# A strided read moves from VectorE and ACT to TensorE: the gated unit of a two-layer trunk

## The chip, the core and the metric

The kernel runs on one core of a Trainium2 chip. The metric is device time in microseconds (us) of one execution. TensorE (PE in the rows; its weight loads PEld) multiplies matrices, VectorE (DVE), ACT and GpSimd (POOL) work on elements, and SyncE (SP) issues most of the DMAs. A tile has 128 partitions and lies in SBUF; results of TensorE come out in PSUM banks of 512 float32 columns.

## What is computed

The program is two residual layers on a (1024 frames, 1024 channels) float32 input. The change is in the first layer, behind its state-space mixer. There `y` is the mixer's output and `gate` the second half of the input projection:

```python
y = jax.nn.gelu(y)
y = y * jax.nn.sigmoid(y @ s5_w_glu[j] + s5_b_glu[j])
out = (y * jax.nn.silu(gate)) @ s5_w_out[j]
x = x + out
```

The second line is the gated unit. Its product with `s5_w_glu` is 1024 x 1024 x 1024, and so is the product with `s5_w_out` that follows.

## The kernel before

Channels lie on partitions, in eight tiles of 128 channels (`KT` = 8), with the 1024 frames in the columns. A float32 matrix product is made of three products of rounded halves: each operand is split into `hi`, its value rounded to the type that TensorE takes at full rate, and `lo`, the rest. `mm3` issues hi by hi, hi by lo and lo by hi as three matmuls of 512 moving columns into one PSUM bank.

The mixer works on chunks of `L` = 8 frames, so it leaves y in another order of columns: in `bh[k]` and `bl[k]` (hi and lo of channel tile k; `hi` and `lo` in the rows) column l*128 + c holds frame c*8 + l. The input `zt` (the gate, stored by frames) and the results `ahi` and `alo` (hi and lo of what goes into the product with `s5_w_out`) are in order of frames, column c*8 + l.

The gated unit is the loop over `i` in 0..7 below (lines 1017 to 1037), each turn with two halves of 512 columns. A half here is l = 0..3 or l = 4..7 with all 128 chunks. One half adds `bh` and `bl` to `yv`, multiplies by silu of the gate (a Sigmoid on ACT and two multiplications on VectorE), takes 24 matmuls in `project` over the eight channel tiles with a slice of `w_glu` as stationary operand, puts a Sigmoid on the bank (ACT), multiplies, rounds to `ahi` (ACT) and subtracts to `alo` (VectorE). `of_frames` is a view of a tile in order of frames that walks it in steps of 8 columns, 32 bytes: it is read for the gate (one ACT and one VectorE instruction), written for `ahi` (ACT), and read and written for `alo` (VectorE). TensorE reads `bh` and `bl` as 512 adjacent columns. `sig`, `zt` and `yv` are `c` in the rows, and `bglu` is the bias.

Before this loop lie the input projection (`mm<-ahi,w_hi` and the like), the mixer and `y_split`, which splits each y tile into `bh` and `bl` half by half. Behind it comes `load_panel`: four DMAs of 512 KB bring a panel of `s5_w_out` into `raw` (two buffers), ACT and VectorE split it into the tiles that held `bh` and `bl`, and `apply_panel` multiplies it with slices of `ahi` and `alo` (`mm<-hi,ahi` in the rows). Up to the loop, instructions keep the order in which they are written; from the loop on a scheduler orders them for each engine. Every engine works its queue in order. All compute instructions are recorded under line 74, the helper that issues them, so they are told apart by tiles.

Of the kernel before, what the change touches and what calls it, by code (L numbers as in the profile page):

```python
# [18 lines left out]
F32 = mybir.dt.float32  # L19
F32R = mybir.dt.float32r  # L20
I32 = mybir.dt.int32
AF = mybir.ActivationFunctionType
ALU = mybir.AluOpType
# [5 lines left out]
KT = D // P  # L29
# [3 lines left out]
L = 8  # L33
# [27 lines left out]
def trunk(ctx, tc, x, norm_g, final_g, s5_w_in, A_re, A_im, log_dt, B_re, B_im, C_re, C_im,  # L61
# [17 lines left out]
    V, S, GP, T, Q = (Engine(e) for e in (nc.vector, nc.scalar, nc.gpsimd, nc.tensor, nc.sync))  # L79
# [20 lines left out]
    def mmps():  # L100
        return bank("mm")

    def auxps():
        return bank("aux")
# [9 lines left out]
    def mm3(ps, a, b, first, last):  # L114
        (ah, al), (bh, bl) = a, b
        T.matmul(ps, lhsT=ah, rhs=bh, start=first, stop=False)
        T.matmul(ps, lhsT=ah, rhs=bl, start=False, stop=False)
        T.matmul(ps, lhsT=al, rhs=bh, start=False, stop=last)

    def sub_hi(eng, lo, src, hi):  # L120
        eng.tensor_tensor(lo, src, hi.bitcast(F32), ALU.subtract)
# [27 lines left out]
    def load_w(src, col0, lo_eng=None, raw=None):  # L149

        if raw is None:
            raw = raw_tile([P, KT, P])
        Q.dma_start(raw, src[:, col0:col0 + P].rearrange("(k p) c -> p k c", p=P))
        hi = wsp.tile([P, KT, P], F32R, name="w_hi", tag="hi")
        lo = wsp.tile([P, KT, P], F32R, name="w_lo", tag="lo")
        S.activation(hi, raw, AF.Copy)
        sub_hi(lo_eng or V, lo, raw, hi)
        return hi, lo

    def project(ps, w, a, half):  # L160
        hi, lo = w
        mh, ml = a
        cs = slice(half * HALF, (half + 1) * HALF)
        for k in range(KT):
            mm3(ps, (hi[:, k], lo[:, k]), (mh(k)[:, cs], ml(k)[:, cs]), k == 0, k == KT - 1)
# [27 lines left out]
    ahi = A.tile([P, KT, D], F32R, name="ahi")  # L193
    alo = A.tile([P, KT, D], F32R, name="alo")
# [495 lines left out]
    b_pool, bh, bl = [], {}, {}  # L690
    c_n = [0]

    def ctile(dt=F32, shape=(P, D)):
        c_n[0] += 1
        return b_pool[1].tile(list(shape), dt, name="c", tag=f"c{c_n[0] % 8}")
# [7 lines left out]
    def b_lo(k):  # L703
        return bl[k]

    def by_l(a):
        return a.rearrange("p (l c) -> p l c", l=L // 2)

    def of_frames(a, half):

        return a.rearrange("p (c l) -> p l c", l=L)[:, half * (L // 2):(half + 1) * (L // 2)]

    def load_y(k):
        bl[k] = btile(k, "lo")
# [301 lines left out]
    b_ops = (b_hi, b_lo)  # L1016
    banks.update(mm=[0, 1, 2, 3], aux=[4, 5, 6, 7])
    for i in range(KT):
        w = w_next
        if i < KT - 1:  # L1020
            w_next = load_w(w_glu[0], (i + 1) * P)
        sig, zt, yv = ctile(), ctile(), ctile()
        Q.dma_start(zt, z_d[i])
        for half in range(2):
            hs = slice(half * HALF, (half + 1) * HALF)

            zs = of_frames(zt, half)
            V.tensor_tensor(yv[:, hs], bh[i][:, hs].bitcast(F32), bl[i][:, hs].bitcast(F32), ALU.add)
            S.activation(by_l(sig[:, hs]), zs, AF.Sigmoid)
            V.tensor_tensor(by_l(yv[:, hs]), by_l(yv[:, hs]), zs, ALU.mult)  # L1030
            V.tensor_tensor(yv[:, hs], yv[:, hs], sig[:, hs], ALU.mult)
            ps = mmps()
            project(ps, w, b_ops, half)
            S.activation(sig[:, hs], ps, AF.Sigmoid, bias=bglu[:, i:i + 1])
            V.tensor_tensor(yv[:, hs], yv[:, hs], sig[:, hs], ALU.mult)
            S.activation(of_frames(ahi[:, i], half), by_l(yv[:, hs]), AF.Copy)
            V.tensor_tensor(of_frames(alo[:, i], half), by_l(yv[:, hs]), of_frames(ahi[:, i], half).bitcast(F32), ALU.subtract)


    gb = late.tile([P, D], F32, name="gb", tag="gb")  # L1040
# [37 lines left out]
    for half in range(2):  # L1078
        hs = slice(half * HALF, (half + 1) * HALF)
# [5 lines left out]
        for n in range(KT):  # L1085
            ps = mmps()
# [39 lines left out]
    for q in range(2):  # L1126
        ps = auxps()
# [11 lines left out]
    for q in range(2):  # L1139
        ps = auxps()  # L1140
# [6 lines left out]
    for half in range(2):  # L1147
# [10 lines left out]
        for n in range(KT):  # L1158
            ns = slice(n * P, (n + 1) * P)
            ps = mmps()  # L1160
# [19 lines left out]
    for h in range(8):  # L1180
        w = w_next
# [4 lines left out]
        for half in range(2):  # L1186
            hs = slice(half * HALF, (half + 1) * HALF)
            ps = mmps()
# [3 lines left out]
            ps = auxps()  # L1192
# [15 lines left out]
    for half in range(2):  # L1208
        hs = slice(half * HALF, (half + 1) * HALF)
# [6 lines left out]
        for n in range(KT):  # L1216
            ps = mmps()
# [39 lines left out]
```

## Time and profile before

| | us |
|---|---|
| time, median of 3 runs (848.52 to 853.45) | 850.79 |
| the profiled execution's own time | 851.53 |
| its span, first to last instruction | 849.8 |
| TensorE busy | 821.2 (97%) |
| VectorE busy | 495.9 (58%) |
| ACT busy | 293.6 (35%) |
| gated unit on TensorE: 384 matmuls | 275.4 to 366.0 |

The span is the time from the first to the last instruction; the profiled time is 1.7 us above it. Busy time of an engine is an average over stages with different limits. The stage of the gated unit is read by a window of its own, from 275.4 to 366.0 us, with the windows on either side of it. In a window's row each engine has its busy time and the count of its instructions, and PEclk is the granted clock of TensorE as a share of full speed.

A matmul's own duration (about 0.4 us) holds the filling and draining of the array, which overlap with its neighbours. What one matmul costs in a stream is the distance from its start to the next one's start.

### The profile page before, as it was taken

How to read it: one execution, taken by the hardware profiler on the slowest of the kernel's cores; microseconds unless marked ns; L12 is line 12 of the kernel's file. 1: busy time of each engine (PE TensorE's matmuls, PEld its weight loads, DVE VectorE, ACT ScalarE, POOL GpSimd, SP SyncE). 2: the span in 40 equal slices, each digit the busy share in tenths (PEclk: the TensorE clock that was granted, in tenths of full speed). 3: DMA queues.
4: the chain of work that ended last, by engine and by line, in shares of the span. 5: the costliest groups of instructions: out<-in, count | busy, mean ns of one | idle time of the engine just before them, and what ended most of it. 6: DMA issues, size and time to landing. Idle time of an engine off the chain costs nothing.

```text
span 849.8 us, 10879 instructions
## 1 busy us (share of the span) xinstructions
PE 821.2 (97%) x3978; PEld 668.1 (79%) x3978; DVE 495.9 (58%) x1035; ACT 293.6 (35%) x519; POOL 192.0 (23%) x197
## 2 busy tenths in 40 slices
PE   7999899999999999989999999999999999999996
PEld 5776688888887788758888888888888888888884
DVE  7889788888625978773177311221398545452255
ACT  5632444444423755563122321311321222332122
POOL 2059777787520000000000000000000112113221
PEclk9999899999999999999999999999999999999998
DMA  9826787878987723374021221200310112270022
GB/s 276 113 74 181 177 224 201 206 203 203 240 181 196 223 75 124 123 224 149 0 99 75 99 75 49 100 25 1 99 51 1 29 46 93 99 250 5 0 100 99
DMA packets 123573, 101.72 MB, mean 120 GB/s; under 512 B 21504, under 2 KB 104448, under 8 KB 123520
## 3 DMA queue, kind: packets, MB, share of 16 engines
q1 hardware_dynamic: 113040, 94.41, 39.9%
q10 hardware_dynamic: 10480, 6.62, 2.5%
q8 instruction: 31, 0.51, 0.3%
q14 instruction: 22, 0.18, 0.1%
HBM read 66.93 MB, written 25.17 MB: 108 GB/s over the span
## 4 chain that ended last, share of the span: by engine, by line
PE 60%; DVE 14%; DMA 10%; ACT 5%; POOL 4%; issue 3%; SPq 3%; DVEq 0%; ACTq 0%; POOLq 0%
PE mm L74 55%; DVE c L74 4%; PE aux L74 4%; SPq L74 3%; DMA raw<-in_s_w_in 3%; ACT c L74 2%; DMA lo<-y_d 2%; DVE stage L74 1%; DVE w_lo L74 1%; DMA t_d<-kpad 1%; DVE rot L74 1%; POOL w_lo L74 1%; DMA raw<-in_s_w_out 1%; ACT w_hi L74 1%; DVE wn L74 1%
## 5 line engine op out<-in xcount | busy, mean ns | idle before, releaser
L74 PE MATMUL mm<-ahi,w_hi 128*128 128x512 f32 x512 | 210.0, 410 | 5.9 <-DVE stage L74 4.4
L74 PE MATMUL mm<-alo,w_hi 128*128 128x512 f32 x512 | 202.7, 396 | 0.0
L74 PE MATMUL mm<-ahi,w_lo 128*128 128x512 f32 x512 | 195.7, 395 | 0.0
L74 PEld LDWEIGHTS mm<-ahi,w_hi 128*128 128x128 f32 x512 | 96.9, 189 | 27.9 <-DVE stage L74 5.7
L74 PEld LDWEIGHTS mm<-ahi,w_lo 128*128 128x128 f32 x512 | 96.7, 189 | 21.4
L74 PEld LDWEIGHTS mm<-alo,w_hi 128*128 128x128 f32 x512 | 97.2, 190 | 19.9 <-DVE alo L74 2.2
L74 DVE TENSOR_TENSOR w_lo<-raw,w_hi 128x1024 fp32r<-128x1024 f32 x28 | 40.8, 1456 | 69.0 <-ACT w_hi L74 69.0
L74 PE MATMUL mm<-c,ahi 128*128 128x512 f32 x256 | 80.4, 396 | 0.0
L74 POOL TENSOR_TENSOR c<-c,hi 128x512 f32<-128x512 f32 x16 | 21.0, 1311 | 258.9 <-ACT c L74 258.9
L74 ACT ACTIVATE w_hi<-raw 128x1024 fp32r<-128x1024 f32 x38 | 40.1, 1056 | 76.1 <-PE mm L74 56.2
L74 DVE TENSOR_TENSOR c<-mm,c 128x512 f32<-128x512 f32 x32 | 21.9, 690 | 65.7 <-PE mm L74 65.7
L74 PEld LDWEIGHTS mm<-c,ahi 128*128 128x128 f32 x256 | 48.0, 188 | 11.5
L74 PE MATMUL mm<-hi,ahi 128*128 128x512 f32 x128 | 51.4, 402 | 3.4 <-ACT hi L74 2.8
L74 POOL TENSOR_SCALAR_AFFINE_SELECT wsn<-wsn 128x1024 f32<-128x1024 f32 x1 | 1.1, 1091 | 230.3 <-DMA wsn<-in_sgu_w_s 230.3
L74 PE MATMUL mm<-hi,w_hi 128*128 128x512 f32 x128 | 50.7, 396 | 1.6 <-ACT w_hi L74 1.6
L74 PE MATMUL mm<-lo,ahi 128*128 128x512 f32 x128 | 51.6, 403 | 0.5 <-DVE lo L74 0.5
L74 PE MATMUL mm<-hi,alo 128*128 128x512 f32 x128 | 51.7, 405 | 0.0
L74 DVE TENSOR_TENSOR c<-c 128x512 f32<-128x512 f32 x64 | 49.5, 815 | 3.2 <-POOL c L74 3.1
L74 PE MATMUL mm<-hi,w_lo 128*128 128x512 f32 x128 | 50.6, 397 | 0.3 <-DVE w_lo L74 0.3
L74 PE MATMUL mm<-ahi,hi 128*128 128x512 f32 x128 | 50.7, 396 | 0.0
L74 PE MATMUL mm<-lo,w_hi 128*128 128x512 f32 x128 | 50.6, 396 | 0.0
L74 PE MATMUL mm<-alo,hi 128*128 128x512 f32 x128 | 50.6, 395 | 0.0
(174 smaller groups left out, 1438.4 us busy)
## 6 DMA issues: line engine op xcount, KB each, us to landing
raw<-in_sgu_w_in SPq DMA_DIRECT2D x24, 512.0 KB, 3.7
cs<-e SPq DMA_DIRECT2D x32, 256.0 KB, 3.9
raw<-in_s_w_in SPq DMA_DIRECT2D x14, 512.0 KB, 5.8
u_d<-stage SPq DMA_DIRECT2D x8, 512.0 KB, 5.3
us<-u_d SPq DMA_DIRECT2D x16, 256.0 KB, 5.2
t_d<-kpad SPq DMA_DIRECT2D x64, 64.0 KB, 3.0
traw<-t_d SPq DMA_DIRECT2D x16, 256.0 KB, 4.9
y_d<-ysb ACTq DMA_DIRECT2D x16, 256.0 KB, 3.3
```

Of the source, the lines that this page charges most:

```text
L74: ins = getattr(self.engine, name)(*args, **kwargs)
```

## The change

The frames are now put in order where TensorE reads y. `frames(a, half)` views a y tile as 64 chunks of 8 frames, the innermost step being 128 columns (512 bytes): a half is now 512 frames in sequence, chunks 0..63 or 64..127 with all eight l. The sum `yv`, the gate, the Sigmoids, the bank, `ahi` and `alo` all lie in order of frames, in adjacent columns. The addition reads `bh` and `bl` with the step of 128 columns. Every one of the 384 matmuls of the loop has such a view as its moving operand; the weights and the output bank stay as they were.

```diff
-    def by_l(a):
-        return a.rearrange("p (l c) -> p l c", l=L // 2)
-
-    def of_frames(a, half):
-
-        return a.rearrange("p (c l) -> p l c", l=L)[:, half * (L // 2):(half + 1) * (L // 2)]
+    def frames(a, half):
+
+        return a.rearrange("p (l c) -> p c l", l=L)[:, half * 64:(half + 1) * 64]
+
+    def by_c(a):
+        return a.rearrange("p (c l) -> p c l", l=L)
...
-            zs = of_frames(zt, half)
-            V.tensor_tensor(yv[:, hs], bh[i][:, hs].bitcast(F32), bl[i][:, hs].bitcast(F32), ALU.add)
-            S.activation(by_l(sig[:, hs]), zs, AF.Sigmoid)
-            V.tensor_tensor(by_l(yv[:, hs]), by_l(yv[:, hs]), zs, ALU.mult)
+            V.tensor_tensor(by_c(yv[:, hs]), frames(bh[i].bitcast(F32), half), frames(bl[i].bitcast(F32), half), ALU.add)
+            S.activation(sig[:, hs], zt[:, hs], AF.Sigmoid)
+            V.tensor_tensor(yv[:, hs], yv[:, hs], zt[:, hs], ALU.mult)
             V.tensor_tensor(yv[:, hs], yv[:, hs], sig[:, hs], ALU.mult)
             ps = mmps()
-            project(ps, w, b_ops, half)
+            for k in range(KT):
+                mm3(by_c(ps), (w[0][:, k], w[1][:, k]), (frames(bh[k], half), frames(bl[k], half)), k == 0, k == KT - 1)
             S.activation(sig[:, hs], ps, AF.Sigmoid, bias=bglu[:, i:i + 1])
             V.tensor_tensor(yv[:, hs], yv[:, hs], sig[:, hs], ALU.mult)
-            S.activation(of_frames(ahi[:, i], half), by_l(yv[:, hs]), AF.Copy)
-            V.tensor_tensor(of_frames(alo[:, i], half), by_l(yv[:, hs]), of_frames(ahi[:, i], half).bitcast(F32), ALU.subtract)
+            S.activation(ahi[:, i, hs], yv[:, hs], AF.Copy)
+            sub_hi(V, alo[:, i, hs], yv[:, hs], ahi[:, i, hs])
```

On TensorE the order of the 384 matmuls is the same in both kernels. It first differs where they end and the panel begins. The names are `hi0` to `hi7` for the panel's tiles by channel tile, and one `mm` for each tile of 128 frames:

```order
 L74 MATMUL mm_3508<-hi7_2925,w_lo_3394 128x512
 L74 MATMUL mm_3581<-hi0_2763,ahi_80 128x512
+L74 MATMUL mm_3609<-hi0_2763,ahi_80 128x512
+L74 MATMUL mm_3637<-hi0_2763,ahi_80 128x512
 L74 MATMUL mm_3581<-lo0_2514,ahi_80 128x512
 L74 MATMUL mm_3581<-hi0_2763,alo_81 128x512
 L74 MATMUL mm_3581<-hi1_2785,ahi_80 128x512
+L74 MATMUL mm_3609<-lo0_2514,ahi_80 128x512
+L74 MATMUL mm_3609<-hi0_2763,alo_81 128x512
 L74 MATMUL mm_3581<-lo1_2589,ahi_80 128x512
 L74 MATMUL mm_3581<-hi1_2785,alo_81 128x512
 L74 MATMUL mm_3581<-hi2_2812,ahi_80 128x512
```

Work of the second and third tile of frames (`mm_3609`, `mm_3637`) now stands among that of the first, before the panel's later tiles are asked for.

On ACT, at the same place, before (`c<-mm,bglu` is a Sigmoid that empties a bank of the gated unit, `hi_2763` to `hi_2925` are the panel's eight tiles):

```order
L74 ACTIVATE c<-mm,bglu 128x512
L74 ACTIVATE hi_2763<-raw 128x512
L74 ACTIVATE hi_2785<-raw 128x512
L74 ACTIVATE ahi<-c 128x4x128
L74 ACTIVATE hi_2812<-raw 128x512
L74 ACTIVATE hi_2835<-raw 128x512
L74 ACTIVATE c<-mm,bglu 128x512
L74 ACTIVATE hi_2856<-raw 128x512
```

and after:

```order
L74 ACTIVATE c<-mm,bglu 128x512
L74 ACTIVATE hi_2763<-raw 128x512
L74 ACTIVATE hi_2785<-raw 128x512
L74 ACTIVATE ahi<-c 128x512
L74 ACTIVATE hi_2812<-raw 128x512
L74 ACTIVATE hi_2835<-raw 128x512
L74 ACTIVATE c<-mm,bglu 128x512
L74 ACTIVATE hi_2856<-raw 128x512
```

The rows stand alike, but before there is one more Sigmoid of the gated unit behind them, and after these two are the last ones: the panel's first copies have moved one half behind, and `ahi` is written in one run of 512 columns.

## Rows read from the trace of the kernel before

**Rows 1.** The page: engine, busy us (share of the span), instructions.
```profile
PE 821.2 (97%) x3978; PEld 668.1 (79%) x3978; DVE 495.9 (58%) x1035; ACT 293.6 (35%) x519; POOL 192.0 (23%) x197
```

**Rows 2.** Windows: start:end, length, busy us (instructions) by engine, granted clock, DMA.
```profile
255.00:275.40 20.40, 18.82 (x81) 14.93 (x79) 10.79 (x18) 6.23 (x11) 0.00 (x0) 1.00 0.74 190
275.40:366.00 90.60, 90.22 (x384) 71.94 (x385) 75.81 (x89) 54.40 (x62) 0.00 (x0) 1.00 0.44 137
366.00:381.00 15.00, 11.06 (x37) 7.11 (x36) 10.00 (x14) 8.32 (x14) 0.00 (x0) 0.89 0.76 246
```

**Rows 3.** Timeline of PE: start us, us, instruction [idle before <- releaser]. Gated unit.
```profile
275.46 0.49 PE L74 MATMUL mm<-hi,w_hi 128*128 128x512 f32 x1 [1.64 <-ACT w_hi L74]
...
278.44 0.40 PE L74 MATMUL mm<-hi,w_hi 128*128 128x512 f32 x1
...
281.01 0.39 PE L74 MATMUL mm<-hi,w_lo 128*128 128x512 f32 x1
```

**Rows 4.** VectorE by shapes, 262 to 385 us: busy us, mean ns, idle before.
```profile
L74 DVE TENSOR_TENSOR alo<-c,ahi 128x512 fp32r<-128x512 f32 x16 | 20.6, 1286 | 6.4 <-ACT ahi L74 6.2
L74 DVE TENSOR_TENSOR w_lo<-raw,w_hi 128x1024 fp32r<-128x1024 f32 x8 | 9.8, 1222 | 18.5 <-ACT w_hi L74 18.5
L74 DVE TENSOR_TENSOR lo<-raw,hi 128x512 fp32r<-128x512 f32 x14 | 9.0, 688 | 6.4 <-ACT hi L74 6.4
L74 DVE TENSOR_TENSOR c<-hi,lo 128x512 f32<-128x512 f32 x13 | 8.5, 689 | 0.2
```

**Rows 5.** ACT by shapes, 262 to 385 us.
```profile
L74 ACT ACTIVATE ahi<-c 128x512 fp32r<-128x512 f32 x16 | 19.9, 1243 | 35.9 <-DVE c L74 35.9
L74 ACT ACTIVATE c<-c 128x512 f32<-128x512 f32 x16 | 19.1, 1257 | 0.0
L74 ACT ACTIVATE w_hi<-raw 128x1024 fp32r<-128x1024 f32 x8 | 8.5, 1059 | 11.0 <-DMA raw<-in_s_w_glu 11.0
L74 ACT ACTIVATE hi<-raw 128x512 fp32r<-128x512 f32 x14 | 8.1, 626 | 8.6 <-DMA raw<-in_s_w_out 8.6
```

**Rows 6.** VectorE: gate's multiplications, 281 to 285 us; input projection's evictions (min/median/max ns), strided, contiguous.
```profile
L74 DVE TENSOR_TENSOR c<-c 128x512 f32<-128x512 f32 x3 | 3.6, 1224 | 0.0
...
L74 DVE TENSOR_TENSOR stage<-mm,rb x13: 664/1132/1183, 63.7 to 171.7; 128x512 f32<-128x512 f32 x13
...
L74 DVE TENSOR_TENSOR stage<-mm,rb x13: 665/680/692, 187.6 to 280.8; 128x512 f32<-128x512 f32 x13
```

**Rows 7.** Timeline behind the gated unit: the first panel's matmuls and what they wait for.
```profile
368.16 0.50 PE L74 MATMUL mm<-lo,ahi 128*128 128x512 f32 x1 [0.30 <-DVE lo L74]
...
371.66 1.15 ACT L74 ACTIVATE hi<-raw 128x512 fp32r<-128x512 f32 x2 [3.92 <-DMA raw<-in_s_w_out]
...
372.34 0.51 PE L74 MATMUL mm<-hi,ahi 128*128 128x512 f32 x1 [2.76 <-ACT hi L74]
...
373.06 0.65 PE L74 MATMUL mm<-lo,ahi 128*128 128x512 f32 x1 [0.22 <-DVE lo L74]
373.51 0.63 PE L74 MATMUL mm<-hi,alo 128*128 128x512 f32 x1
...
375.22 0.63 PE L74 MATMUL mm<-hi,ahi 128*128 128x512 f32 x1
...
376.70 0.40 PE L74 MATMUL mm<-hi,ahi 128*128 128x512 f32 x1
...
379.61 0.50 PE L74 MATMUL mm<-hi,ahi 128*128 128x512 f32 x1 [0.66 <-ACT ahi L74]
```

**Rows 8.** Timelines at the loop's start: the last y tiles' splits on ACT and VectorE.
```profile
275.31 3.22 ACT L74 ACTIVATE hi<-lo 128x512 fp32r<-128x512 f32 x6
...
278.39 2.49 DVE L74 TENSOR_TENSOR lo<-lo,hi 128x512 fp32r<-128x512 f32 x4
```

## The prediction

> **What bounds the kernel now.** I read the page's table of engines first: TensorE is busy 97% of the span, VectorE 58%, ACT 35% [rows 1]. An average doesn't say which engine sets the end of the gated unit, so I read three windows next [rows 2]. In the stage of 90.60 us TensorE is busy for 90.22 with 384 matmuls at full granted clock (PEclk 1.00, the upper level, 2.4 GHz); VectorE is busy for 75.81 and ACT for 54.40. So TensorE is the bound there: 0.4 us of the stage is left to win by making the others faster. Behind it, from 366 to 381 us, TensorE has 3.9 us without work and a granted clock of 0.89. The timeline of TensorE gives the price of one matmul [rows 3]: from the start at 278.44 to the one at 281.01 us lie eleven steps, 2.57 / 11 = 0.2336 us for 512 columns, or 0.456 ns a column. 384 x 0.2336 = 89.7 us is the stage. Whatever the change does to this one number is multiplied by 384; all else in it happens on engines with slack.
>
> **The change part by part.** *VectorE and ACT lose strides.* Groups of one operation with and without a step of 8 columns show what a stride costs them. VectorE's subtraction to `alo` takes 1286 ns, the same subtraction on adjacent columns 688 [rows 4]; the multiplication by the gate takes 1224 [rows 6]. ACT's rounding to `ahi` takes 1243 and the gate's Sigmoid 1257, against 626 on adjacent columns [rows 5]. The change takes from VectorE 16 x (1.286 - 0.688) + 16 x (1.224 - 0.688) = 18.1 us, and from ACT 16 x 0.617 + 16 x 0.631 = 20.0 us. It gives VectorE a stride in the 16 additions of `bh` and `bl`, now 689 ns [rows 4]; at the excess of 0.6 us just seen that is 9.6 us back. No row has a step of 128 columns; from 0.45 us (the evictions below) to twice 0.6 for two strided inputs, 7 to 19 us, so VectorE's own balance is between -11 and +1 us. None of this is on the path within the stage, because TensorE fills it: the price of these edits there is nothing, and TensorE's 90.22 us is the cover. It shows only at the two ends of the stage.
>
> *The end of the stage.* The waits of TensorE behind it are 0.30, 2.76, 0.22 and 0.66 us, 3.9 together, the longest for a panel tile that ACT could copy only when a DMA of `s5_w_out` had landed [rows 7]. After the 2.76 us without work matmuls start about 0.43 us apart (373.51 to 375.22, four steps), which is the lower level of 1.2 GHz, until the row at 376.70: nine steps from 372.34 in 4.36 us against 2.1 at full clock, of which 0.2 is a wait already counted, so 2.0 more. Together up to 5.9 us. The panel's tiles overwrite the y tiles, so ACT may copy one only once TensorE has read that y tile for the last time. If TensorE reads y slowly, the DMAs run ahead of it and these waits nearly go; I take -5 us, from bounds of 0 and -5.9. The order shown ahead, in which work of a second and third tile of frames fills the wait for the later panel tiles, points the same way.
>
> *The start.* A half now needs both halves of every y tile. The last tiles are split until 275.31 + 3.22 = 278.53 on ACT and 278.39 + 2.49 = 280.88 on VectorE [rows 8], and TensorE comes to the eighth tile 21 matmuls after 275.46, at about 280.4. That is 0 to 0.5 us of new waiting, and nothing when matmuls take longer.
>
> *TensorE gains a stride.* This decides. All moving operands of TensorE in the kernel before are adjacent columns, so no row shows the price of 512 columns at a step of 128. What rows show is the price of a strided column on the two other engines. ACT: 512 columns more cost 1059 - 626 = 433 ns, 0.85 ns a column, and the stride adds 617 or 631 ns on 512, so 2.05 or 2.08 ns a strided column [rows 5]. VectorE: (1222 - 688) / 512 = 1.04 ns a column, plus 598 / 512 = 1.17, so 2.21 ns; for the gate's multiplication 1.04 + 536 / 512 = 2.09 [rows 4, 6]; for the evictions of the input projection, the same operation in two layouts, 1.04 + (1132 - 680) / 512 = 1.93 [rows 6]. Two engines whose adjacent columns differ by a fifth (0.85 and 1.04) meet at about 2 ns when each column is fetched apart. The rows look like a time of the memory and not of the engine. If so, TensorE pays it too: 512 x 1.93 to 512 x 2.21 is 0.988 to 1.132 us for a matmul instead of 0.2336. Of these I take the lowest, 1.93, since TensorE is the fastest reader here (0.456 ns). The term is 384 x (0.988 - 0.2336) = 290 us; with 2.21 it is 345.
>
> The Trainium skill ("SBUF — State Buffer", section "Door 1: The DMA port swizzle") says that the memory has lines of 16 bytes, that full bandwidth wants at least two accesses in a row to one line, and that each step to a new line pays. That it pays, the rows of VectorE and ACT bear out; the size of the penalty and TensorE's part in it the page doesn't give. Read with this case's rate, four adjacent columns to a line, 4 x 0.456 = 1.82 ns a line and one line a column, it would make a matmul 0.934 us, an estimate, and the kernel 851.5 + 384 x 0.700 - 5 = 1115 us.
>
> **The sum.** Against the profiled execution's own 851.5 us: + 290 (384 matmuls) - 5 (end of the stage) + 0 (start) = 1136 us. The median of the runs is 0.7 us lower than that execution, which does not count here.
>
> **The rivals.**
> *A, the forecast: a time per fetched column.* 1136 us at 1.93 ns, 1191 at 2.21, 1197 without the gain at the end. For it: two engines with different rates meet at the same nanoseconds. Against it: TensorE may have a wider path to the memory than the other two.
> *B, a factor.* A strided column costs each engine a multiple of its own adjacent column: 1.93 / 1.04 = 1.85 to 2.08 / 0.85 = 2.45 in the rows above. Then a matmul takes 0.432 to 0.572 us, the stage gains 76 to 130 us, and the kernel takes 923 to 977 us, near 945 at 2.1. For it: both engines lose roughly half their rate. Against it: the factors differ (2.0 and 2.45) where the nanoseconds agree.
> *C, a sum.* The stride adds a fixed excess to the instruction, 0.452 to 0.631 us in the rows; 384 of them are 174 to 242 us, and the kernel takes 1020 to 1089. It fits the same rows, but a matmul is pipelined with the next, so an addition that ignores the engine's own rate is the least natural of the three.
> *D, not slower: TensorE takes strided columns at its own rate.* The place is the moving operand of the 384 matmuls, the price 0 per column. The 90.6 us stage stays, the stage's end gives 0 to 5.9 us, the start takes up to 0.5, and the kernel takes 846 to 852 us, 849 in the middle. It decides from a matmul longer by less than 5.9 / 384 = 0.015 us, 6%. For it: nothing in the trace shows TensorE limited by its operand's layout. Against it: the only two engines seen with strides both pay, and TensorE asks for a column twice as often as they do. The Trainium skill ("TensorE: Matmul & The Clock Gate", section "Step-by-step: what each phase is for") states such a rule: throughput is purely the number of columns, one fed in each cycle. The trace agrees for adjacent columns to within a tenth, 0.456 ns against a cycle of 0.417; no run here shows it for strided ones.
>
> That the change doesn't do what it says holds in part: VectorE still has 16 strided instructions of its former 32. It would move the time only in D.
>
> **How the numbers follow.** A 50%, B 25%, C 8%, D 15%, and 2% for something outside, such as a step of 128 columns costing far more than one of 8. The predicted time is A's. The range goes from B's lower end to A's upper, 923 to 1197 us; it holds A, B and C, 83%. About 0.5%, 4.3 us, is what a measurement of this kernel can tell from no change. A, B and C are slower by far more, 85% with the rest. D is split by its own bounds: most of 846 to 852 lies within 4.3 us of 850.8, so 11% for no change and 4% for faster.
>
> **What would show it.** Right: the distance between starts of the 384 matmuls near 1 us, the stage near 380 us, TensorE still the one without idle time in it, `alo<-c,ahi` near 690 ns and both ACT groups near 630 on the engines that now wait for TensorE, the addition `c<-hi,lo` near 1.2 us, and the waits behind the stage nearly gone. A distance of 0.43 to 0.57 us is B, 0.69 to 0.87 is C, 0.234 is D. A granted clock below 1.00 in the stage would mean that TensorE, waiting for columns, is also throttled; where the memory sets the rate it changes nothing, and in B it would hide as a doubling. The forecast is wrong if TensorE fetches several strided columns at once.

## The result, and the profile after

The changed kernel takes 941.37 us (median; 937.82 to 941.49) against 850.98 us before: a ratio of 1.1059, 95% interval 1.1033 to 1.1085. It is slower, as forecast, by 90 us and not by 285: the time of rival B. The profiled execution took 937.82 us, 1.7 more than its span of 936.1; the other three took 941.35 to 941.49.

The page's table of engines and three windows of the changed kernel, which answer to [rows 1, 2] (columns as there):

```profile
PE 914.1 (98%) x3978; PEld 676.9 (72%) x3978; DVE 489.2 (52%) x1035; ACT 278.0 (30%) x519; POOL 192.2 (21%) x197
...
255.00:272.12 17.12, 17.12 (x77) 14.05 (x75) 10.34 (x14) 4.96 (x10) 0.00 (x0) 1.00 0.70 188
272.12:459.08 186.96, 186.96 (x385) 80.33 (x384) 70.97 (x94) 42.05 (x63) 0.00 (x0) 1.00 0.24 76
459.08:474.00 14.92, 14.92 (x65) 12.03 (x64) 7.49 (x12) 6.28 (x13) 0.00 (x0) 1.00 0.53 178
```

All of the 90 us and more lies in the middle row. The gated unit takes 186.96 us where it took 90.60, at a granted clock of 1.00 in both, with TensorE busy throughout. In the rows on either side TensorE has no idle time now, where before it had 1.6 and 3.9 us.

The timeline of TensorE in that stage gives the price of a matmul, as in [rows 3]:

```profile
272.12 0.71 PE L74 MATMUL mm<-hi,w_hi 128*128 128x512 f32 x1
...
278.53 0.69 PE L74 MATMUL mm<-hi,w_lo 128*128 128x512 f32 x1
...
283.89 0.69 PE L74 MATMUL mm<-lo,w_hi 128*128 128x512 f32 x1
```

From 278.53 to 283.89 lie eleven steps: 0.487 us for a matmul, 2.08 times the 0.2336 of before, and 0.951 ns a column. 384 x (0.487 - 0.2336) = 97 us.

VectorE and ACT, by shapes from 262 to 475 us (answers to [rows 4, 5]):

```profile
L74 DVE TENSOR_TENSOR c<-hi,lo 128x512 f32<-128x512 f32 x12 | 15.4, 1320 | 0.2
L74 DVE TENSOR_TENSOR alo<-c,ahi 128x512 fp32r<-128x512 f32 x16 | 10.9, 684 | 2.1 <-ACT ahi L74 1.4
...
L74 ACT ACTIVATE ahi<-c 128x512 fp32r<-128x512 f32 x16 | 10.3, 646 | 13.9 <-DVE c L74 13.9
L74 ACT ACTIVATE c<-c 128x512 f32<-128x512 f32 x16 | 9.1, 631 | 0.0
```

Their strides are gone and their instructions take half as long, except the addition of hi and lo, which took the stride over (689 to 1320 ns).

The account against the profiled execution of before: the stage from its first to its last matmul +96.4 (186.96 against 366.06 - 275.46 = 90.60); ahead of it -3.3 (it begins at 272.12, not 275.46, of which 1.64 is the wait in [rows 3]); behind it -6.7 (477.0 us from its end to the end of the span, before 483.7). Together +86.3, and the spans differ by 936.1 - 849.8 = 86.3. The -3.3 ahead of the stage belongs to this execution more than to the change: its first matmul of the input projection begins at 11.0 us and not at 12.4, in code that both kernels share, and the other three executions are 3.5 us longer.

### The profile page after: what moved, and what is told of

It is laid out like the page before. It is cut to its first block, busy times and chain, and to the rows that moved or that the text cites. A ratio compares the mean times of both kernels' runs of the same rounds, so it can differ in the third digit from the quotient of the medians.

```text
span 936.1 us, 10879 instructions
## 1 busy us (share of the span) xinstructions
PE 914.1 (98%) x3978; PEld 676.9 (72%) x3978; DVE 489.2 (52%) x1035; ACT 278.0 (30%) x519; POOL 192.2 (21%) x197
## 4 chain that ended last, share of the span: by engine, by line
PE 80%; DVE 7%; DMA 5%; POOL 4%; ACT 2%; SPq 1%; issue 1%; DVEq 0%; ACTq 0%; POOLq 0%
PE mm L74 75%; PE aux L74 4%; DMA raw<-in_s_w_in 2%; SPq L74 1%; DVE gg L74 1%; DVE rot L74 1%; POOL w_lo L74 1%; DVE stage L74 1%; POOL hh L74 1%; DMA cs<-e 1%; POOL e L74 1%; POOL et L74 1%; POOL s L74 1%; DVE tv L74 1%; DVE t L74 1%
## 5 line engine op out<-in xcount | busy, mean ns | idle before, releaser
L74 PEld LDWEIGHTS mm<-ahi,w_lo 128*128 128x128 f32 x512 | 96.4, 188 | 21.1
L74 PE MATMUL mm<-lo,w_hi 128*128 128x512 f32 x128 | 88.1, 689 | 0.0
L74 PE MATMUL mm<-hi,w_hi 128*128 128x512 f32 x128 | 88.1, 688 | 0.0
L74 PE MATMUL mm<-hi,w_lo 128*128 128x512 f32 x128 | 87.9, 688 | 0.0
L74 DVE TENSOR_TENSOR c<-c 128x512 f32<-128x512 f32 x64 | 41.8, 682 | 59.8 <-ACT c L74 56.6
L74 PEld LDWEIGHTS mm<-hi,w_lo 128*128 128x128 f32 x128 | 26.8, 209 | 35.5 <-issue 35.2
L74 PEld LDWEIGHTS mm<-lo,w_hi 128*128 128x128 f32 x128 | 26.8, 209 | 35.4 <-issue 35.1
L74 PEld LDWEIGHTS mm<-hi,w_hi 128*128 128x128 f32 x128 | 26.8, 209 | 35.3 <-issue 35.3
```

Of the source, the lines that this page charges most:

```text
L74: ins = getattr(self.engine, name)(*args, **kwargs)
```

## The experiments

Where a kernel below mixes columns of the product with the gate of other frames, its output is not the reference's; its work has the same size, and only its time is used. `pe_only`, `cold` and the eight kernels with other steps and runs were executed once each; the kernel before scattered from 848 to 853 us.

**Which half of the change costs.** One kernel strides TensorE's reads alone, another eases VectorE and ACT alone.

```diff
 # pe_only, from the kernel before
-            project(ps, w, b_ops, half)
+            for k in range(KT):
+                mm3(by_c(ps), (w[0][:, k], w[1][:, k]), (frames(bh[k], half), frames(bl[k], half)), k == 0, k == KT - 1)
...
 # elem_only, from the changed kernel
-            for k in range(KT):
-                mm3(by_c(ps), (w[0][:, k], w[1][:, k]), (frames(bh[k], half), frames(bl[k], half)), k == 0, k == KT - 1)
+            project(ps, w, b_ops, half)
```

> The kernel before, with the 384 matmuls of the gated unit reading y in steps of 128 columns as in the changed kernel; VectorE and ACT keep their views in steps of 8 columns (so columns of the product and of the gate no longer belong to the same frame). Theory 1, the loss is TensorE's reading alone: starts of matmuls 0.4865 us apart as in the changed kernel, 384 x (0.4865 - 0.2336) = 97 us on the stage, and a time of 937 to 945 us, because VectorE and ACT, strided or not, hide under a stage of 187 us. Rival: their work matters still, and with their strides kept the time is longer than the changed kernel's by part of the 30 us that they save, 945 to 970 us.

> The changed kernel, with the 384 matmuls reading 512 adjacent columns as before; VectorE and ACT keep the changed kernel's views (so the product's columns are in another order than the gate's). Theory 1, TensorE alone carries the loss and the eased engines give back only the waits at the two ends of the stage: matmuls 0.2336 us apart and 843 to 850 us. Rival: the eased engines give nothing, since the end waits for a DMA of the panel anyway: 850 to 853 us. A second rival, that the changed kernel's other edits cost time: above 854 us.

Measured: 943.54 us with TensorE's stride alone, and 843.73 us with the other half alone, ratio 0.9918 (0.9896 to 0.9941). So the loss is TensorE's reading, all of it. Strided or not, VectorE and ACT make no difference that can be seen under a stage of 187 us: the span of `pe_only` is 5.7 us longer than that of the changed kernel's profiled execution (941.8 against 936.1), and its stage begins 5.65 us later (277.77 against 272.12), 2.4 of them a wait for the first weights, so that nothing is left for the stage and what follows. Without TensorE's stride their relief is worth 0.8%. Window 366 to 381 us of the second kernel, where the kernel before had 11.06 us of work in 15 [rows 2]:

```profile
366.00:381.00 15.00, 15.00 (x66) 12.06 (x65) 8.61 (x14) 7.03 (x14) 0.00 (x0) 1.00 0.76 243
```

66 matmuls in the time of 37, at full clock: the 6.3 us that the kernel gained (849.98 to 843.73) are the waits behind the stage and the half clock that followed them, up to 5.9 us in the prediction's count.

**A time or a factor.** The changed kernel with TensorE made idle ahead of the stage:

```diff
     w_next = in_w[16]
+    for _ in range(8):
+        S.activation(w_next[0], w_next[0].bitcast(F32), AF.Copy)
```

> The changed kernel, with eight more copies of the first weight tile onto itself on ACT ahead of the gated unit (8 x 1.06 us), so that TensorE sits idle for some 8 us and begins its strided matmuls at the lower granted clock, 1.2 GHz. Theory E, the price belongs to TensorE and scales with its clock: the first matmuls start 0.97 us apart, twice 0.4865, and fall to 0.4865 once the clock is back. Theory M, the price is a time of the memory, 0.95 ns a column: they start 0.4865 us apart, or a little more, from the first one on, at half clock too. The total is 8 to 10 us over the changed kernel under M, 2 to 6 us more under E.

Measured: 948.99 us, 7.6 over the changed kernel's median. Windows (the clock is the third number from the end) and the timeline of TensorE behind the idle time:

```profile
282.80:284.00 1.20, 1.18 (x2) 0.88 (x3) 1.20 (x3) 1.20 (x1) 0.00 (x0) 0.50 1.02 410
286.00:287.00 1.00, 1.00 (x4) 0.64 (x3) 1.00 (x3) 1.00 (x3) 0.00 (x0) 0.50 1.15 333
290.00:294.00 4.00, 4.00 (x9) 1.66 (x8) 0.00 (x0) 3.65 (x4) 0.00 (x0) 1.00 0.02 4
```

```profile
282.82 0.87 PE L74 MATMUL mm<-hi,w_hi 128*128 128x512 f32 x1 [8.32 <-ACT w_hi L74]
...
286.34 0.67 PE L74 MATMUL mm<-lo,w_hi 128*128 128x512 f32 x1
286.83 0.67 PE L74 MATMUL mm<-hi,w_lo 128*128 128x512 f32 x1
287.31 0.67 PE L74 MATMUL mm<-hi,w_hi 128*128 128x512 f32 x1
...
291.69 0.67 PE L74 MATMUL mm<-hi,w_hi 128*128 128x512 f32 x1
292.18 0.67 PE L74 MATMUL mm<-lo,w_hi 128*128 128x512 f32 x1
```

At half the granted clock matmuls start 0.485 us apart (286.34 to 287.31, two steps), at full clock 0.49 (291.69 to 292.18). The first steps behind the idle time hold three longer ones (0.69, 0.64 and 0.71 us), at the start and around a wait for the first low weights. Theory M holds for the step of 128 columns: its price doesn't follow the granted clock. It is a time; that it is spent on the way from the memory to the array is inferred, and no row shows the place. Adjacent columns behind a wait pay for the lost clock (0.43 us each in [rows 7]) where these strided ones don't. The total is just under the 8 to 10 us that theory M was given.

**Which step, which run.** In the first three kernels below every view of the loop, TensorE's included, has one step s in columns. `step8_short` keeps the step of 8 and lets TensorE walk it in runs of 8 columns in place of 128. In the other four TensorE alone walks y in runs of j adjacent columns before each jump of 128.

```diff
 # step2, step4, step8: STEP = 2, 4, 8, from the kernel before
-        return a.rearrange("p (c l) -> p l c", l=L)[:, half * (L // 2):(half + 1) * (L // 2)]
+        return a.rearrange("p (c l) -> p l c", l=STEP)[:, half * (STEP // 2):(half + 1) * (STEP // 2)]
...
-            project(ps, w, b_ops, half)
+            for k in range(KT):
+                mm3(by_l(ps), (w[0][:, k], w[1][:, k]), (of_frames(bh[k], half), of_frames(bl[k], half)), k == 0, k == KT - 1)
...
 # step8_short: TensorE's view, the others as in step8
+        return a.rearrange("p (o n l) -> p o l n", n=8, l=L)[:, :, half * 4:(half + 1) * 4]
...
 # pairs, run4, run64: j = 2, 4, 64, TensorE's view in the changed kernel (run4's line)
+        return a.rearrange("p (l c j) -> p c l j", l=L, j=4)[:, half * 16:(half + 1) * 16]
...
 # run4_off: the same, shifted by two columns
+        return a.rearrange("p (l c) -> p l c", l=L)[:, :, 2 + half * 60:66 + half * 60].rearrange("p l (c j) -> p c l j", j=4)
```

> The kernel before, with the matmuls of the gated unit reading y in steps of 8 columns (32 bytes), the step that VectorE and ACT use there, in place of adjacent columns (columns of the product and of the gate no longer belong together). Theory 1, a column costs the same once it is fetched apart, whatever the step: starts 0.4865 us apart and 937 to 945 us. Rival, the step of 512 bytes is dearer than one of 32 bytes, or cheaper: another distance, 0.35 to 0.45 us or 0.55 to 1.0 us, with 384 times the difference in the total.

> The kernel before, with every view in steps of 8 columns (gate, ahi, alo) now in steps of 2 columns (8 bytes), and the matmuls of the gated unit reading y in steps of 2 as well, 512 of a tile's 1024 columns (columns no longer belong to the right frames). Theory P, TensorE's read side fetches two adjacent columns at a time, some 0.84 ns a fetch, so any step over 1 halves the rate: matmuls 0.43 us apart as with steps of 8, total near 917 us. Theory L, it fetches 16 bytes, and two columns of the four are enough: 0.234 to 0.26 us apart, total 845 to 855. For VectorE and ACT: if they pay as with steps of 8, alo and the gate's multiplication 1.2 to 1.3 us; if two columns of four are enough for them, 0.69 us, and 0.63 on ACT.

> The same with steps of 4 columns (16 bytes). Theory P and theory L both expect 0.43 us between matmuls and a total near 917 us; a memory that fetches 32 bytes or more at a time would give less, 0.25 to 0.40 us, as steps of 8 then reach the full price and steps of 4 do not. VectorE and ACT: 1.2 to 1.3 us if their price, too, is one for a column fetched apart.

> The run with steps of 8 columns in the matmuls, with the same columns walked in another order: 64 runs of 8 columns in steps of 8, in place of 4 runs of 128. Steps of 128 columns gave 0.4865 us, steps of 8 gave 0.431, but the first also had 64 runs of 8 and the second 4 runs of 128. Theory R, what the 0.055 us between them pays is the start of each inner run, 0.055 / 60 = 0.9 ns for one: 0.4865 us apart, total near 938 us. Theory S, it pays the longer step: 0.431 us, total near 917 us.

> The changed kernel, with the matmuls reading two adjacent columns (chunks c and c+1 of one l) before each jump of 128 columns, so 256 runs of 2 in place of single columns (columns of the product and of the gate no longer belong together). Theory P, two adjacent columns are one fetch: 0.234 us apart without a price for the start of a run, and with 0.9 ns for each of 256 starts (theory R) 0.234 + 0.23 = 0.46 us; the total 845 or near 930 us. Rival, each jump costs whatever the columns ahead of it: 0.35 us, half of what single columns cost above adjacent ones, and a total near 890 us.

> The changed kernel, with the matmuls reading four adjacent columns (16 bytes) before each jump of 128 columns (columns of the product and of the gate no longer belong together). Steps of 2, 4, 8 and 128 columns and pairs of adjacent columns all cost TensorE 0.43 to 0.49 us. Theory F, TensorE has a fast way to read, two columns at a time, only for a long adjacent run, and any jump drops it to one column per 0.84 ns: 0.43 to 0.49 us here too, total 917 to 941 us. Theory G, it reads 16 bytes at a time, and the four columns of a run come together: 0.234 to 0.30 us, total 843 to 870 us.

> The same with runs of 64 adjacent columns, eight of them in a half (frames by chunk halves, not in sequence). Theory F, if the length of the run decides: near 0.24 us with eight jumps of about 1 ns, total 843 to 850 us. Rival, that the shape of the view decides (a moving operand with more than one dimension is read column by column): 0.43 us or more, total near 917 us.

> The run with four adjacent columns (16 bytes) before each jump, shifted by two columns: each run now begins 8 bytes past a multiple of 16 (columns of the product and of the gate do not belong together, and four chunks are read in both halves). Theory A, what counts is the place in memory, a group of 16 bytes that is read at once: a run now touches two groups and has two columns in each, like the run with pairs, so 0.43 to 0.49 us between matmuls, total 917 to 943 us. Theory B, what counts is that four columns follow each other in the view, wherever they start: 0.28 us as before, total 860 to 864 us.

Measured, the distance between starts of matmuls in the stage, read as above over several steps of each timeline from about 319 us on (the first row is that of [rows 3]; its total is a median of four executions, and that of the change too):

| moving columns | us a matmul | ns a column | total us |
|---|---|---|---|
| 512 adjacent (before) | 0.2336 | 0.456 | 850.98 |
| step 2 (8 bytes) | 0.473 | 0.924 | 935.28 |
| step 4 (16 bytes) | 0.461 | 0.900 | 931.54 |
| step 8, runs of 128 | 0.431 | 0.842 | 917.33 |
| step 8, runs of 8 | 0.432 | 0.844 | 920.93 |
| step 128 (the change) | 0.487 | 0.951 | 941.37 |
| pairs, then a jump of 128 | 0.487 | 0.951 | 941.77 |
| four adjacent, then a jump | 0.279 | 0.545 | 862.10 |
| the same, 8 bytes off | 0.490 | 0.957 | 941.62 |
| 64 adjacent, then a jump | 0.233 | 0.455 | 841.71 |

The rows of the timeline behind four of them, in this order: step 2 (eleven steps), pairs (twelve), four adjacent columns on a multiple of 16 bytes, and four 8 bytes off it:

```profile
319.33 0.65 PE L75 MATMUL mm<-lo,w_hi 128*128 128x512 f32 x1
...
324.53 0.65 PE L75 MATMUL mm<-hi,w_hi 128*128 128x512 f32 x1
```

```profile
319.02 0.67 PE L74 MATMUL mm<-lo,w_hi 128*128 128x512 f32 x1
...
324.87 0.67 PE L74 MATMUL mm<-lo,w_hi 128*128 128x512 f32 x1
```

```profile
319.75 0.44 PE L74 MATMUL mm<-hi,w_hi 128*128 128x512 f32 x1
...
323.10 0.44 PE L74 MATMUL mm<-hi,w_hi 128*128 128x512 f32 x1
```

```profile
319.76 0.68 PE L74 MATMUL mm<-hi,w_lo 128*128 128x512 f32 x1
...
323.19 0.67 PE L74 MATMUL mm<-hi,w_hi 128*128 128x512 f32 x1
```

The last two decide: twelve steps in 3.35 us on the multiple, seven in 3.43 off it. So theory A of the last expectation: four columns cost TensorE 1.8 ns (4 x 0.456) to 2.2 (4 x 0.545) together, as if taken at once, if they are the four of one 16-byte place in memory and follow each other in the view. In every other order that was run each column costs 0.84 to 0.96 ns, as if taken by itself. That one place is one fetch is the reading of these times; no row shows a fetch, and runs of 3, of 8 or longer ones off the multiple were not run. Two of a group of four aren't enough, whether they lie side by side (pairs) or apart (step 2). The length of the runs at a step of 8 is nothing (0.431 and 0.432), so the 0.055 us between steps of 8 and 128 belong to the step; steps of 2 and 4 lie in between, and what makes them differ stays open. A step of 8 also costs what adjacent columns cost at half the granted clock (0.431 and 0.43 us), and no run tells whether that is more than chance. Of the expectations, `step8` came out as its rival, a cheaper step. `step2` and `step4` had the right side with the wrong size, 0.46 and 0.47 us for 0.43. `pairs` met none of its theories (0.234, 0.46 or 0.35 us): two adjacent columns are not one fetch. `step8_short` (theory S), `run4` (theory G) and `run64` came out as one of theirs said.

The same kernels show that VectorE and ACT have another rule. Steps of 2 (the first two rows) and of 4, by shapes from 262 to 460 us:

```profile
L75 DVE TENSOR_TENSOR alo<-c,ahi 128x512 fp32r<-128x512 f32 x16 | 11.0, 689 | 2.3 <-ACT ahi L75 1.5
...
L75 ACT ACTIVATE ahi<-c 128x512 fp32r<-128x512 f32 x16 | 10.8, 674 | 14.0 <-DVE c L75 14.0
```

```profile
L75 DVE TENSOR_TENSOR alo<-c,ahi 128x512 fp32r<-128x512 f32 x16 | 18.0, 1126 | 6.7 <-ACT ahi L75 6.7
...
L75 ACT ACTIVATE ahi<-c 128x512 fp32r<-128x512 f32 x16 | 18.6, 1163 | 14.5 <-DVE c L75 14.5
```

A step of 2 columns is free for VectorE (689 against 688 ns) and nearly so for ACT (674 against 626), and costs TensorE a factor of two. A step of 4 costs the two 1126 and 1163 ns, about as much as one of 8 (1096 and 1140 in `step8`). Two accesses to one line of 16 bytes, which the Trainium skill ("SBUF — State Buffer", section "Door 1: The DMA port swizzle") asks for full bandwidth, are enough for VectorE and ACT here; for TensorE the measurement differs, it wants all four in sequence.

**A kernel faster than both.** `elem_only` leaves the product's columns in another order than the gate's, but adjacent columns on every engine can be had. The y tiles are split anyway, by one ACT and one VectorE instruction a half. If the splits read the tile in steps of 128 columns and write `bh` and `bl` in order of frames, nothing in the loop has a stride, TensorE's reads included. The low part then needs a tile of its own, one more than before.

```diff
 # once and once_early: in y_split, with the changed kernel's adjacent views in the loop, and project as before
-            S.activation(bh[k][:, hs], bl[k][:, hs].bitcast(F32), AF.Copy)
-            sub_hi(V, bl[k][:, hs], bl[k][:, hs].bitcast(F32), bh[k][:, hs])
+            S.activation(by_c(bh[k][:, hs]), frames(y, half), AF.Copy)
+            V.tensor_tensor(by_c(lo[:, hs]), frames(y, half), by_c(bh[k][:, hs]).bitcast(F32), ALU.subtract)
...
 # once and defer: the split of the first w_glu tile behind all y tiles
-        split(V)
+        if splits and splits[0] < 16:
+            split(V)
...
 # once_early and early: its DMA from ACT's queue, ahead of later y tiles
-        Q.dma_start(in_raw[i], src[:, col:col + P].rearrange("(k p) c -> p k c", p=P))
+        (S if i == 16 else Q).dma_start(in_raw[i], src[:, col:col + P].rearrange("(k p) c -> p k c", p=P))
```

> The kernel before, with the split of the first gated unit's weights moved behind the splits of all y tiles, so that on ACT and VectorE the last y tiles no longer queue behind a weight tile whose DMA lands at 274 us. If only the start of the stage is touched: 0 to 2 us less than before, 848 to 851 us.

> A kernel that keeps TensorE's adjacent columns and still eases VectorE and ACT in the stage: the splits of the y tiles write bh and bl in order of frames (ACT and VectorE read the tile in steps of 128 columns there, 16 instructions each, ahead of the stage), with the weights' split moved as in the run that does only that; the loop then has no stride at all. If the 0.8% that the run with adjacent matmuls and eased engines gained can be had in a kernel that computes the reference's function: 841 to 845 us, matmuls 0.234 us apart, and hardly a wait behind the stage. Rival: the strided splits come late, TensorE waits for the last y tile, and the gain is lost: 847 to 852 us.

> The kernel before, with the DMA of the first gated unit's weights issued from ACT's queue, ahead of the copies of the later y tiles, and no longer behind 28 DMAs of y on SP's queue. If the wait of 1.64 us at the start of the stage is the late landing of these weights: TensorE enters the stage without it, 847 to 850 us. Rival, it waits for the last y tile instead: 849 to 852 us.

> Both: the y tiles put in order of frames where they are split, so that neither TensorE nor the loop has a stride, the weights' split at its old place, and their DMA issued early. The run with the first alone lost its gain to a wait of 3.3 us and half clock after it, as the low part of the first weights stood behind the last strided splits on VectorE. With these weights early: no wait at either end of the stage, 839 to 844 us. Rival: the last y tile is late now, its strided splits queued on VectorE until some 2 us into the stage, 845 to 850 us.

Measured against the runs of before on the same chip: `defer` 852.85 us, 1.0014 (0.9996 to 1.0032); `once` 849.60, 0.9994 (0.9979 to 1.0010); `early` 852.39, 1.0028 (1.0012 to 1.0044); `once_early` 842.62, 0.9901 (0.9880 to 0.9921). The first two bring nothing, `early` costs 0.3%, the last one saves 1%; the gains expected of `defer`, `once` and `early` did not come. What TensorE waits for from 262 to 385 us (us in total, times, longest) shows why, first in `once`, then in `early`; in `once_early` no row is left:

```profile
PE mm L74 <- ACT w_hi L74: 4.2, 2, 3.3
```

```profile
PE mm L74 <- DVE w_lo L74: 2.3, 3, 1.2
PE mm L74 <- ACT hi L74: 2.1, 1, 2.1
PE mm L74 <- ACT ahi L74: 0.7, 1, 0.7
PE mm L74 <- DVE lo L74: 0.5, 2, 0.3
PE mm L74 <- ACT w_hi L74: 0.3, 1, 0.3
```

With the y tiles in order but the first weights' split behind them, a wait moved to the start of the stage. With the weights early but the loop still strided, the first wait went (the last input matmul at 274.83 and the first one of the unit at 275.05 follow each other) and others came: for the next low weights, which VectorE makes, and for the panel as before. `once_early`, which has the y tiles in order, the early weights and their split at its old place, leaves TensorE without a wait, as three windows show, to be read against [rows 2].

```profile
255.00:272.00 17.00, 17.00 (x76) 13.96 (x75) 17.00 (x20) 12.56 (x12) 0.00 (x0) 1.00 0.77 167
272.00:362.00 90.00, 89.93 (x387) 72.03 (x386) 62.34 (x92) 42.91 (x63) 0.00 (x0) 1.00 0.50 161
362.00:381.00 19.00, 19.00 (x83) 15.32 (x82) 10.69 (x17) 9.39 (x18) 0.00 (x0) 1.00 0.76 252
```

VectorE is as busy as 17.00 of 17.00 us just ahead of the stage, where the strided splits now run (1097 ns each), and has 62.34 us of work in the stage, before 75.81. The y tiles in order with the split at its old place and the DMA as before were not run, so how much of the 1% is the earlier DMA's stays open.

## Why the prediction was wrong

*What bounds the stage.* Right: TensorE, with no idle time in 187 us; 384 times the change of one number is the result.

*VectorE and ACT.* Right in the sizes: 684 ns, 646 and 631 where about 690 and 630 were expected, and 1320 for the addition, an excess of 0.63 us inside the bounds of 0.45 to 1.2. Right in the place too: `pe_only` shows that the relief moves nothing under the longer stage. The addition was expected near 1.2 us and is a tenth above it.

*The end of the stage.* -5 from bounds of 0 and -5.9; the account has -6.7 behind the stage. The waits there are gone; 0.8 us more than the bound went, and the runs don't say where. The prediction's reason, that TensorE reads slowly and the DMAs run ahead, is enough for it (`pe_only`, strided VectorE and ACT, has no wait there) but not needed: `elem_only` has none either, with TensorE at full rate. So in rival D the gain would have come too, 843.73 us, below the 846 to 852 that D was given: its gain behind the stage was undervalued by some 2 us.

*The start.* Expected at 0 to +0.5, measured -3.3. The wait for the first weights (1.64 us before) is absent in the profiled execution of the changed kernel, 2.4 us in `pe_only`, 1.8 in `elem_only`. It hangs on the landing of one DMA and was not the change's doing as far as the runs show: it is absent in `step8` too, whose loading and splitting of y and of the weights are those of the kernel before. That a slow TensorE would hide the late splits of the last y tiles held.

*TensorE's stride, the step that failed.* The prediction saw that strided columns on two engines cost about the same 2 ns, took it for a time of the memory that all readers share ("If so, TensorE pays it too"), and put 1.93 ns on TensorE (up to 2.21): 290 us. It was 0.951 ns and 97 us. The estimate of one 16-byte line for each column, 1.82 ns and 1115 us, failed in the same way. That no shared time stands behind it is shown by `step2`: a step that VectorE and ACT hardly feel (689 and 674 ns) doubles TensorE's time. The agreement of the two engines was also not the constant that it seemed. With TensorE reading at step 8, 0.431 us a matmul, the same `alo` subtraction took 1096 ns in place of 1286 and the rounding to `ahi` 1140 in place of 1243, so their price in [rows 4, 5] changed with what TensorE was reading. Within `step8` the pairs before and after TensorE went back to adjacent columns, at 438.64 us, show the same:

```profile
431.63 1.12 ACT L75 ACTIVATE ahi<-c 128x512 fp32r<-128x512 f32 x1
432.78 1.08 DVE L75 TENSOR_TENSOR alo<-c,ahi 128x512 fp32r<-128x512 f32 x1 [0.33 <-ACT ahi L75]
...
440.54 1.26 ACT L75 ACTIVATE ahi<-c 128x512 fp32r<-128x512 f32 x1
441.83 1.28 DVE L75 TENSOR_TENSOR alo<-c,ahi 128x512 fp32r<-128x512 f32 x1 [0.30 <-ACT ahi L75]
```

TensorE's rate alone doesn't set it: in `pe_only`, with TensorE slower still but at a step of 128, the two took 1208 and 1218 ns on average. And the splits of `once_early`, which read at a step of 128, took 1097 ns on VectorE and 1150 on ACT while TensorE read adjacent columns. What makes the difference stays open.

*Kind and size.* The kind, a time and not a factor of the engine's own clock, held, on TensorE alone (`cold`). Rival B gave the right total, 945 at a factor of 2.1 against 2.08 measured, and its lower end set the range's; that the measured time lies inside the range is B's doing. But B's total was right by luck of the full clock: its reason, a multiple of the engine's rate, doesn't hold at half the granted clock, where the factor is 0.485 / 0.43 = 1.13. C's 0.69 us and D's 0.234 are ruled out by the timeline. The sign that the prediction named for being wrong, that TensorE fetches several strided columns at once, did not come either: it pays for each strided column, only half of what was forecast.

*The weights.* The text had one row against its own favourite, TensorE's rate of 0.456 ns a column, four times faster than the 1.93 ns it was given; it named a wider path as an objection to A, but used the rate only as a reason for the lower end of 2 ns and gave a read path of TensorE's own no term in the sum. With that objection open, 50% for A was too much.

## What to carry to other kernels

Price a strided operand on the engine that will read it: a row of another engine tells that strides cost something, not how much. For TensorE's moving operand of 4-byte columns, keep runs of at least four on a 16-byte place (0.279 us a matmul of 512 columns with runs of four, 0.233 with runs of 64); every other order that was run costs 0.43 to 0.49. If an order has to change, do it once where a tile is written anyway and not in an operand that is read eight times over by the bounding engine, and then look at what the step displaces in its own queue: here the reorder gained nothing with the weights' split put off (`once`), and 1% with the split in its place and an earlier DMA (`once_early`).

## What was not expected of the hardware

- Two adjacent columns before a jump cost TensorE as much as single ones (0.951 ns a column), and four columns that straddle two 16-byte places too (0.957); four on one place cost 0.545.
- At half the granted clock a stream at a step of 128 columns ran as fast as at the full one (0.485 and 0.49 us a matmul).
- ACT's and VectorE's strided instructions took 8% and 15% less time when TensorE read with a step of 8 columns (1140 and 1096 ns against 1243 and 1286), but only 2% and 6% less when it read with a step of 128 (1218 and 1208). The cause wasn't isolated.
